# Spreading the S5 Toeplitz tables by SBUF-to-SBUF DMAs from GpSimd instead of one-hot matmuls

## The chip, the cores and the metric

The kernel runs on one core of one Trainium2 chip. The metric is the device time of one execution in microseconds, taken as the median over runs. Beside the timed runs there is one profiled execution, and all rows below come from it.

## What is computed

The reference is a two-layer decoder trunk on 256 positions of width 2048. Layer 0 is an S5 state-space mixer, layer 1 a sparse-attention mixer; both sit between RMS norms with modulation by a vector c. Only the S5 mixer matters here:

```python
u, z = jnp.split(h @ w_in, 2, axis=-1)
ug = u.reshape(B_, L, SSM_GROUPS, SSM_GROUP)        # 128 groups of 16 channels
bu = einsum('blgc,gnc->blgn', ug, bb)               # complex, 64 states per group
x  = scan over l of  x_l = a * x_{l-1} + bu_l       # complex, diagonal
y  = Re(einsum('blgn,gcn->blgc', x, c)) + d_skip * ug
y  = gelu(y); y = y * sigmoid(y @ w_glu + b_glu)
out = (y * silu(z)) @ w_out
```

The scan is cut into blocks of four positions. What the positions of one block do to each other is a small lower-triangular Toeplitz matrix per group (4 by 4 blocks of 16 by 16 numbers). Its first block row, 16 by 64 numbers per group, is the table this case is about.

## The kernel before

Weights stream from DRAM in 512 KB pieces into a ring of eight slots (`raw`, loads issued from SyncE's queue). `split_w` (lines 194 to 206) makes of each half piece a rounded part `hi` on ScalarE (line 203) and a remainder `lo` on VectorE (line 204), and `project_half` (lines 222 to 230) runs three matmuls of 128x256 per weight tile on them, at lines 228, 229 and 230, into the tile `acc`. All large projections go this way.

The S5 mixer interleaves its own work with such projections. `PLAN` is a list of strings, one for each call of `fill()`: "u" is half a projection of u (24 matmuls), "z" half of one of z, "m" a modulation column pair on TensorE and "d" one on VectorE (line 145, two instructions of 128x1024 each on `raw`). The order in the program is `u_turn(0)`, `scan_in(0)`, `scan_run(0)`, `scan_local(0)`, the rest of the u halves, `u_turn(1)`, `scan_in(1)`, `scan_out(0)`, `scan_run(1)`, `scan_local(1)`, `y_turn(0)`, `scan_out(1)`, `y_turn(1)`; the index is the half f of the groups. The framework then lays the instructions of each engine out by when their operands become ready in its model, not strictly in program order; each engine runs its own list in order.

Before them, in a loop over `s` in the order 2, 3, 0, 1, the tables are made: matmuls at line 482 into `kp`, then `kdt[s // 2]` is put together at lines 486, 487 and 491. `kdt[0]` lies in `ey[:, 2048:2560]`, `kdt[1]` in `stab[:, 0:512]`; each holds eight column groups m of 64 numbers. `scan_local(f)` (lines 658 to 679) has for each `g2` two steps. First the table is spread over partitions: for each `hl`, four one-hot matmuls (line 668, lhsT a window of `sel`, 32 rows deep, 128x512 at the widest) write `tzp` in PSUM, and ScalarE copies it (line 670) into `tz`, which lies in `scr` and has one buffer of 128 x 2 x 8 x 64 numbers. Then 32 small matmuls per `hl` (line 676, `tp`) apply `tz` to `U`, and ScalarE writes the result back into `U` (line 678). A `fill()` follows. `sel` is built on GpSimd at lines 433 and 435.

Around it: `scan_run(f)` (lines 627 to 656) is a chain of VectorE operations at lines 634 to 637 and 655 to 656. `cact`, which line 145 reads, is loaded by GpSimd's queue (line 534) and passed through Silu on ScalarE (line 535). `pick` (lines 537 and 538) and `turn` (line 542) are one-hot tables that GpSimd builds; `u_turn` (line 556) needs `pick`. `load_ct(1)` (line 624) loads 2 MB through GpSimd's queue for `scan_out(1)`.

Of the kernel before, what the change touches and what calls it, by code (L numbers as in the profile page):

```python
# [11 lines left out]
AF = mybir.ActivationFunctionType  # L12
# [60 lines left out]
def trunk_kernel(ctx, tc, xT, crow, ccol, vec, m0n, mn, mt, w_ur, w_in, w_glu, w_out, w_kv, w_qr, w_q, w_g,  # L73
                 w_z, w_o, cw1, cw2, b2row, lam, lstep, bmat, cmat, dvec, outT):
    nc = tc.nc
# [13 lines left out]
    def psb(shape, name):  # L89
        return ps2.tile(shape, F32, tag="sm", name=name)  # L90
# [35 lines left out]
    stab = pool.tile([128, 2112], F32, tag="stab", name="stab")  # L126
# [297 lines left out]
    id32 = stab[:, 1920:1952]  # L424
# [3 lines left out]
    V.tensor_reduce(par, id32.rearrange("p (e c) -> p e c", e=2), axis=AX.X, op=OP.add)  # L428
    id16 = stab[:, 1856:1872]
    V.tensor_add(id16, id32[:, 0:16], id32[:, 16:32])  # L430

    sel = stab[:, 640:816]
    nc.gpsimd.memset(sel, 0.0)
    for e in range(2):
        nc.gpsimd.tensor_copy(sel[:, 48 + 64 * e:64 + 64 * e], id32[:, 16 * e:16 * e + 16])
    kdt = [ey[:, 2048:2560], stab[:, 0:512]]
    kdt = [t.rearrange("p (m n) -> p m n", m=8) for t in kdt]

# [16 lines left out]
    for s in (2, 3, 0, 1):  # L455
# [19 lines left out]
        for x in range(4):  # L475
            for g2 in range(2):
                pr = slice(64 * g2, 64 * g2 + 64)
                for ql in range(2):
                    h = 2 * x + ql
                    o = 64 * g2 + 32 * ql  # L480
                    for r in range(2):
                        nc.tensor.matmul(kp[o:o + 32, x].rearrange("p b m -> p (b m)"),
                                         bb[r][pr, 32 * h:32 * h + 32], kc_[pr, 2 * h:2 * h + 2, r, :],
                                         start=(x == 0 and r == 0), stop=True, skip_group_check=True)
# [8 lines left out]
        for q in range(4):  # L493
            p = psb([128, 2, 2, 128], "btp")
# [17 lines left out]
    tz = scr[:, 2944:3968].rearrange("p (l m n) -> p l m n", l=2, m=8)  # L512

    def powers():
        for t, a in zip(QW, (PR, PI)):
            V.tensor_copy(t[:, 0, :], a[:, :, 3])
        for n in (1, 2, 4):
            d = [[t[:, n + x, :] for t in QW] for x in range(n)]
            for x in range(0, n):
                ar, ai = [t[:, x, :] for t in QW]  # L520
                br, bi = [t[:, n - 1, :] for t in QW]
                u1, u2 = w1[:, 0:64], w2_[:, 0:64]
                V.tensor_mul(u1, ar, br)
                V.tensor_mul(u2, ai, bi)
                V.tensor_sub(d[x][0], u1, u2)
                V.tensor_mul(u1, ar, bi)
                V.tensor_mul(u2, ai, br)
                V.tensor_add(d[x][1], u1, u2)
        for t, i in zip(SG, (0, 7)):
            V.tensor_scalar(t[:, 0, :], QW[1][:, i, :], -1.0, None, op0=OP.mult)  # L530
            V.tensor_copy(t[:, 1, :], QW[1][:, i, :])

    powers()
    nc.gpsimd.dma_start(cact, crow.to_broadcast((128, D)))
    nc.scalar.activation(cact, cact, AF.Silu)
# [57 lines left out]
    def fill():  # L593
        for c in PLAN[slot[0]]:
            {"u": u_half, "z": z_half, "m": pe_mod, "d": dve_mod, "c": lambda: cmp_next(), "q": lambda: q_rows()}[c]()
        slot[0] += 1
# [61 lines left out]
    def scan_local(f):  # L658

        bs = slice(8 * f, 8 * f + 8)  # L660
        kt = kdt[f].rearrange("p m (d c) -> p m d c", d=4)
        for g2 in range(2):
            for hl in range(2):

                pr = slice(64 * g2 + 32 * hl, 64 * g2 + 32 * hl + 32)
                p = psb([128, 8, 4, 16], "tzp")
                for j in range(4):
                    nc.tensor.matmul(p[:, :, j:4, :], sel[pr, 48 - 16 * j:176 - 16 * j], kt[pr, :, 0:4 - j, :],
                                     start=(j == 0), stop=(j == 3), skip_group_check=True)
                nc.scalar.activation(tz[:, hl], p.rearrange("p m j c -> p m (j c)"), AF.Copy)  # L670
            for hl in range(2):
                p = psb([128, 8, 64], "tp")
                for m in range(8):
                    for e in range(2):
                        pr = slice(64 * e, 64 * e + 64)
                        nc.tensor.matmul(p[pr, m, :], tz[pr, hl, m, :], U[pr, 8 * f + m, 2 * g2 + hl, :],
                                         start=(m == 0), stop=True, skip_group_check=True)
                nc.scalar.activation(U[:, bs, 2 * g2 + hl, :], p, AF.Copy)
            fill()

    def scan_out(f, cts):
# [35 lines left out]
    scan_in(0)  # L717
    scan_run(0)
    scan_local(0)
    fill()  # L720
    fill()
# [4 lines left out]
    scan_out(0, load_ct(0))  # L726
    scan_run(1)
    scan_local(1)
    y_turn(0)
    yhl = Act(["va", "vb"], "yhl")  # L730
# [147 lines left out]
    def cmp_next():  # L878
        e, i = divmod(ncmp[0], 4)
        if e < 2 and nblk[0] >= 4 * e + 4:  # L880
            cmp_piece(e, i)
            ncmp[0] += 1
# [5 lines left out]
    def q_rows():  # L888
        k = nrow[0]
        if k == KT or ncmp[0] < 8:  # L890
            return
        nrow[0] += 1
        if k == 0:
            hq[0] = Act(["ha"], "hq")
            qacc.extend([psb([128, 2, L], "qacc%d" % i) for i in range((QN + 1) // 2)])
        while npe[0] < NA + min(NB, 2 * k + 2):
            pe_mod()
        if 2 * k >= NB:
            while ndve[0] < 48 - NA + 2 * k + 2 - NB:
                dve_mod()  # L900
            c = modv[:, 48 + k:65 + k:16]
            V.tensor_add(c, c, modw[:, 16 + k:33 + k:16])
            V.tensor_add(c, c, vecs[:, VOFF["mb"][0] + 48 + k:VOFF["mb"][0] + 65 + k:16])
        V.scalar_tensor_tensor(scol1[:, k:k + 1], in0=modv[:, 64 + k:65 + k], scalar=1.0, in1=vv_("g1", k, k + 1),
                               op0=OP.add, op1=OP.mult)
        norm_mod(x, rstd1, scol1, modv[:, 48:64], hq[0], (k,))
        r = raw_tile("qraw")
        nc.sync.dma_start(r[:, 0:QN, :], w_qr[k].rearrange("p (a b) -> p a b", b=128))
        w = split_w(r, QN)
        for i in range(QN):  # L910
            hi, lo = w[i // 4]
            acc = qacc[i // 2][:, i % 2, :]
            nc.tensor.matmul(acc, hi[:, i % 4, :], hq[0](0, k), start=(k == 0 and i % 2 == 0), stop=False,
                             skip_group_check=True)
            nc.tensor.matmul(acc, hi[:, i % 4, :], hq[0](1, k), start=False, stop=False, skip_group_check=True)  # L915
            nc.tensor.matmul(acc, lo[:, i % 4, :], hq[0](0, k), start=False, stop=(k == KT - 1),
                             skip_group_check=True)
# [38 lines left out]
    for h in range(4):  # L956
# [8 lines left out]
        for k in range(4):  # L965
            kt = 4 * h + k
# [5 lines left out]
    p = psb([128, 2, 48], "gp")  # L972
# [15 lines left out]
    for h in range(16):  # L988
        kv = h // 4
        pn = []  # L990
        for qh in range(2):
# [17 lines left out]
            for br in range(2):  # L1009
                o = 16 + n * br  # L1010
# [64 lines left out]
    for m in range(0, 16, 2):  # L1075
        e = nc.gpsimd if m in (6, 12) else V
# [91 lines left out]
```

## Time and profile before

| what | value |
|---|---|
| median of 3 runs | 1360.05 us (1359.97 to 1362.2) |
| profiled execution, its own time | 1356.18 us |
| its span (first to last instruction) | 1354.5 us |
| busy: TensorE matmul, VectorE, ScalarE, GpSimd | 1267.1, 1056.9, 688.1, 21.7 us |
| `scan_local(0)` and `scan_local(1)` begin | 189.7 and 284.8 us |

PE is TensorE's matmul row, PEld its weight loads, DVE VectorE, ACT ScalarE, POOL GpSimd, SP SyncE. Times in rows are microseconds from the span's start unless marked ns. "L668" is line 668 of the kernel. A releaser behind an arrow is what ended an idle time. PEclk is the clock that was granted to TensorE as a share of 2.4 GHz; 0.5 is 1.2 GHz. Successive matmuls overlap, so the distance from one group's start to the next group's start says more than a duration.

### The profile page before, as it was taken

How to read it: one execution, taken by the hardware profiler on the slowest of the kernel's cores; microseconds unless marked ns; L12 is line 12 of the kernel's file. 1: busy time of each engine (PE TensorE's matmuls, PEld its weight loads, DVE VectorE, ACT ScalarE, POOL GpSimd, SP SyncE). 2: the span in 40 equal slices, each digit the busy share in tenths (PEclk: the TensorE clock that was granted, in tenths of full speed). 3: DMA queues.
4: the chain of work that ended last, by engine and by line, in shares of the span. 5: the costliest groups of instructions: out<-in, count | busy, mean ns of one | idle time of the engine just before them, and what ended most of it. 6: DMA issues, size and time to landing. Idle time of an engine off the chain costs nothing.

```text
span 1354.5 us, 31620 instructions
## 1 busy us (share of the span) xinstructions
PE 1267.1 (94%) x12526; PEld 1203.9 (89%) x12526; DVE 1056.9 (78%) x2291; ACT 688.1 (51%) x1463; POOL 21.7 (2%) x47
## 2 busy tenths in 40 slices
PE   2799999999889999998999899999999999999995
PEld 1678888888789999997999899999999999999995
DVE  5999769799768787659997878777888777776665
ACT  3345543437435555445455445555555565555653
POOL 2000000000100000000000000000000000000001
PEclk9899998999899999997999999999999999999998
DMA  9799954545879899869998789876555444444541
GB/s 342 259 384 316 350 194 147 212 138 197 295 280 362 299 344 327 309 232 385 322 352 272 241 278 326 273 253 216 175 199 192 149 154 145 154 143 154 187 157 62
DMA packets 93253, 331.05 MB, mean 244 GB/s; under 512 B 12512, under 2 KB 12672, under 8 KB 92080
## 3 DMA queue, kind: packets, MB, share of 16 engines
q1 hardware_dynamic: 91792, 321.45, 67.8%
q0 software_dynamic: 1312, 7.58, 1.5%
q8 instruction: 98, 1.61, 0.5%
q14 instruction: 51, 0.42, 0.1%
HBM read 324.79 MB, written 4.19 MB: 243 GB/s over the span
## 4 chain that ended last, share of the span: by engine, by line
PE 62%; DMA 4%; DVE 3%; issue 1%; ACT 1%; DVEq 0%; ACTq 0%
PE acc L230 18%; PE acc L229 18%; PE acc L228 18%; DMA raw<-in_mt_dram 3%; PE s L1002 1%; DVE lo L204 1%; PE op L1053 1%; PE macc L158 1%; PE op L1050 1%; DMA raw<-in_w_kv_dram 1%; DVE raw L145 1%; PE op L1054 1%; PE cp L838 0%; PE qacc L915 0%; PE cp L839 0%
## 5 line engine op out<-in xcount | busy, mean ns | idle before, releaser
L203 ACT ACTIVATE hi<-raw 128x512 fp32r<-128x512 f32 x640 | 400.0, 630 | 450.7 <-PE acc L229 388.6
L204 DVE TENSOR_TENSOR lo<-raw,hi 128x512 fp32r<-128x512 f32 x640 | 433.2, 688 | 154.5 <-ACT hi L203 148.2
L229 PE MATMUL acc<-hq,hi 128*128 128x256 f32 x960 | 274.6, 286 | 0.0
L228 PE MATMUL acc<-hq,hi 128*128 128x256 f32 x960 | 273.1, 285 | 0.4 <-ACT hi L203 0.4
L230 PE MATMUL acc<-hq,lo 128*128 128x256 f32 x960 | 271.0, 284 | 1.5 <-DVE lo L204 1.3
L145 DVE SCALAR_TENSOR_TENSOR raw<-raw,ey 128x1024 f32<-128x1024 f32 x156 | 189.9, 1220 | 63.0 <-DMA raw<-in_mt_dram 57.3
L229 PEld LDWEIGHTS acc<-hq,hi 128*128 128x128 f32 x960 | 181.0, 189 | 3.7 <-issue 3.3
L230 PEld LDWEIGHTS acc<-hq,lo 128*128 128x128 f32 x960 | 180.4, 189 | 3.5 <-DVE lo L204 2.1
L228 PEld LDWEIGHTS acc<-hq,hi 128*128 128x128 f32 x960 | 181.0, 189 | 1.2 <-issue 0.7
L230 PE MATMUL acc<-h,lo 128*128 128x256 f32 x384 | 112.3, 294 | 9.4 <-DVE lo L204 9.3
L230 PE MATMUL acc<-hkv,lo 128*128 128x256 f32 x384 | 112.3, 293 | 4.5 <-DVE lo L204 4.3
L228 PE MATMUL acc<-hkv,hi 128*128 128x256 f32 x384 | 112.0, 292 | 0.9 <-ACT hi L203 0.9
L228 PE MATMUL acc<-h,hi 128*128 128x256 f32 x384 | 112.8, 294 | 0.0
L229 PE MATMUL acc<-hkv,hi 128*128 128x256 f32 x384 | 111.0, 289 | 0.0
L229 PE MATMUL acc<-h,hi 128*128 128x256 f32 x384 | 110.2, 287 | 0.0
L230 PEld LDWEIGHTS acc<-h,lo 128*128 128x128 f32 x384 | 74.5, 195 | 12.4 <-DVE lo L204 11.4
L230 PEld LDWEIGHTS acc<-hkv,lo 128*128 128x128 f32 x384 | 76.1, 198 | 6.1 <-DVE lo L204 5.8
L158 PE MATMUL macc<-mraw,cz 128*32 128x128 f32 x1600 | 56.5, 292 | 24.4 <-DMA mraw<-in_m0n_dram 19.8
L228 PEld LDWEIGHTS acc<-hkv,hi 128*128 128x128 f32 x384 | 76.4, 199 | 1.5 <-ACT hi L203 1.5
L228 PEld LDWEIGHTS acc<-h,hi 128*128 128x128 f32 x384 | 74.6, 194 | 2.9 <-issue 0.8
L229 PEld LDWEIGHTS acc<-hkv,hi 128*128 128x128 f32 x384 | 76.4, 199 | 0.0
L229 PEld LDWEIGHTS acc<-h,hi 128*128 128x128 f32 x384 | 74.7, 195 | 0.0
(339 smaller groups left out, 2808.3 us busy)
## 6 DMA issues: line engine op xcount, KB each, us to landing
raw<-in_mt_dram SPq DMA_DIRECT2D x156, 512.0 KB, 5.8
raw<-in_w_z_dram SPq DMA_DIRECT2D x96, 512.0 KB, 3.8
mraw<-in_m0n_dram SPq DMA_DIRECT2D x64, 512.0 KB, 8.0
raw<-in_w_in_dram SPq DMA_DIRECT2D x48, 512.0 KB, 5.3
raw<-in_w_kv_dram SPq DMA_DIRECT2D x48, 512.0 KB, 6.2
mraw<-in_mn_dram SPq DMA_DIRECT2D x36, 512.0 KB, 6.1
raw<-in_w_glu_dram SPq DMA_DIRECT2D x32, 512.0 KB, 6.6
raw<-in_w_out_dram SPq DMA_DIRECT2D x32, 512.0 KB, 5.9
```

Of the source, the lines that this page charges most:

```text
L145: nc.vector.scalar_tensor_tensor(out=rf, in0=rf, scalar=1.0, in1=cact[:, 1024 * e:1024 * e + 1024], op0=OP.mult, op1=OP.mult, accum_out=mo ...
L158: nc.tensor.matmul(acc[32 * j:32 * j + 32, 128 * e:128 * e + 128], cz[:, q, :], r[:, q % 8, :], start=(e == 0 and q < 4), stop=(q >= 12), ...
L203: nc.scalar.activation(hi[:, 0:c, :], rr, AF.Copy)
L204: nc.vector.tensor_sub(lo[:, 0:c, :], rr, hi[:, 0:c, :].bitcast(F32))
L228: nc.tensor.matmul(acc, hi[:, kk, :], act(0, k), start=(k == 0), stop=False)
L229: nc.tensor.matmul(acc, hi[:, kk, :], act(1, k), start=False, stop=False)
L230: nc.tensor.matmul(acc, lo[:, kk, :], act(0, k), start=False, stop=(k == KT - 1))
L1002: nc.tensor.matmul(sp, qo(a, h)[:, qs], kk[:, kv, b, o:o + w], start=(i == 0), stop=(i == 2))
L1050: nc.tensor.matmul(op_, vc[0:15, kv, :], tcm[0:15, :], start=True, stop=True)
L1053: nc.tensor.matmul(op_, vt[:, kv, br - 1, 0, :], t[:, 0:256], start=True, stop=False)
L1054: nc.tensor.matmul(op_[:, 128:256], vt[:, kv, br - 1, 1, :], t[:, 256:384], start=False, stop=True)
```

## The change

The one-hot matmuls, their PSUM tile and its copy on ScalarE go, and with them `sel`. In their place `load_tz(f, g2)` issues 16 DMAs from GpSimd's queue (two `hl`, two `e`, four `j`); each copies 16 partitions of the table to 16 partitions of `tz`, shifted right by 16 j columns. `tz` is cleared once. The runs are 256, 192, 128 and 64 bytes long for j = 0 to 3, eight of them per partition (for j = 0 they lie one behind the other on both sides). The first load is issued before `powers()`, each later one after the `tp` matmuls that read the tables before it, into the same buffer. `u_turn` stays as it is.

```diff
-    sel = stab[:, 640:816]
-    nc.gpsimd.memset(sel, 0.0)
-    for e in range(2):
-        nc.gpsimd.tensor_copy(sel[:, 48 + 64 * e:64 + 64 * e], id32[:, 16 * e:16 * e + 16])
...
+    nc.gpsimd.memset(tz, 0.0)
+
+    def load_tz(f, g2):
+
+        for hl in range(2):
+            for e in range(2):
+                i = 64 * g2 + 32 * hl + 16 * e
+                for j in range(4):
+                    o = 64 * e + 16 * j
+                    nc.gpsimd.dma_start(tz[o:o + 16, hl, :, 16 * j:64], kdt[f][i:i + 16, :, 0:64 - 16 * j])
+
+    load_tz(0, 0)
     powers()
     nc.gpsimd.dma_start(cact, crow.to_broadcast((128, D)))
...
-        kt = kdt[f].rearrange("p m (d c) -> p m d c", d=4)
         for g2 in range(2):
-            for hl in range(2):
-
-                pr = slice(64 * g2 + 32 * hl, 64 * g2 + 32 * hl + 32)
-                p = psb([128, 8, 4, 16], "tzp")
-                for j in range(4):
-                    nc.tensor.matmul(p[:, :, j:4, :], sel[pr, 48 - 16 * j:176 - 16 * j], kt[pr, :, 0:4 - j, :],
-                                     start=(j == 0), stop=(j == 3), skip_group_check=True)
-                nc.scalar.activation(tz[:, hl], p.rearrange("p m j c -> p m (j c)"), AF.Copy)
             for hl in range(2):
...
                 nc.scalar.activation(U[:, bs, 2 * g2 + hl, :], p, AF.Copy)
+            if 2 * f + g2 < 3:
+                load_tz(f + g2, 1 - g2)
             fill()
```

## Rows read from the trace of the kernel before

**Rows 1.** The page's head: span, and busy time of each engine.
```profile
span 1354.5 us, 31620 instructions
PE 1267.1 (94%) x12526; PEld 1203.9 (89%) x12526; DVE 1056.9 (78%) x2291; ACT 688.1 (51%) x1463; POOL 21.7 (2%) x47
```
**Rows 2.** Busy time by stretch: us, busy (instructions) of each engine, clock, DMA share, GB/s.
```profile
189.72:246.23 56.51, 53.71 (x463) 49.37 (x462) 55.66 (x102) 23.03 (x42) 0.00 (x0) 0.91 0.52 174
284.75:340.93 56.18, 55.45 (x580) 48.88 (x579) 52.69 (x99) 35.92 (x59) 0.00 (x0) 0.97 0.53 192
```
**Rows 3.** Who waited for whom, 160 to 341 us: total, times, longest.
```profile
PE acc L230 <- DVE lo L204: 3.5, 4, 2.4
```
**Rows 4.** Busy time by stretch, columns as in Rows 2: a group of `scan_in`, then around the spreads.
```profile
179.95:181.79 1.84, 1.84 (x66) 1.77 (x65) 0.92 (x2) 0.89 (x2) 0.00 (x0) 1.00 0.50 191
...
189.72:193.68 3.96, 3.96 (x17) 2.47 (x16) 3.92 (x7) 1.49 (x3) 0.00 (x0) 1.00 0.43 141
193.68:196.47 2.79, 2.79 (x13) 2.56 (x12) 2.75 (x6) 0.70 (x2) 0.00 (x0) 0.52 0.50 176
...
198.80:203.26 4.46, 4.46 (x40) 4.32 (x37) 4.36 (x8) 1.87 (x4) 0.00 (x0) 1.00 0.01 3
...
189.72:198.80 9.08, 9.08 (x93) 7.29 (x93) 8.98 (x16) 3.32 (x6) 0.00 (x0) 0.81 0.53 174
203.26:212.34 9.08, 9.08 (x94) 7.29 (x93) 8.98 (x16) 3.32 (x6) 0.00 (x0) 0.81 0.35 113
284.75:293.83 9.08, 9.08 (x93) 7.29 (x93) 8.87 (x18) 3.32 (x6) 0.00 (x0) 0.81 0.68 262
298.30:305.88 7.58, 7.58 (x93) 5.89 (x92) 7.42 (x14) 3.74 (x7) 0.00 (x0) 1.00 0.43 141
```
**Rows 5.** Line 670 on ScalarE, its instructions and durations (ns min/median/max).
```profile
L670 ACT ACTIVATE scr<-tzp x8: 590/598/605, 192.2 to 302.4; 128x512 f32<-128x512 f32 x8
```
**Rows 6.** Line 145 alone in the first stretch of Rows 2: us, DVE busy (instructions).
```profile
189.72:246.23 56.51, 12.05 (x20) 0.91 0.52 174
```
**Rows 7.** GpSimd in order of time: start, us, line, operation [idle before <-releaser].
```profile
2.11 1.06 POOL L130 DMA_DIRECT2D stab<-in_lstep_dram  x2
...
53.83 2.05 POOL L435 COPY stab<-stab 128x16 f32<-128x16 f32 x2
72.47 0.58 POOL L466 DMA_DIRECT2D ctd<-ctA  x1 [16.60 <-DVE ctA L453]
...
143.86 0.35 POOL L537 MEMSET stab<- 128x272 f32 x1
...
282.32 1.06 POOL L624 DMA_DIRECT2D ct<-ctd  x2 [137.66 <-issue]
```
**Rows 8.** DMA issues on GpSimd's queue: count, KB each, median us from issue to landing.
```profile
ct<-ctd POOLq DMA_DIRECT2D x2, 1024.0 KB, 8.7
...
l<-in_cw_dram POOLq DMA_DIRECT2D x1, 128.0 KB, 2.4
...
stab<-in_lstep_dram POOLq DMA_DIRECT2D x2, 16.0 KB, 5.9
```
**Rows 9.** VectorE in order of time, where `kdt[0]` is finished.
```profile
142.81 0.22 DVE L516 COPY scr<-stab 128x64 f32<-128x64 f32 x1 [1.38 <-PE kp L482]
...
161.89 1.22 DVE L145 SCALAR_TENSOR_TENSOR raw<-raw,ey 128x1024 f32<-128x1024 f32 x1 [1.43 <-ACT ey L535]
...
163.04 0.22 DVE L491 TENSOR_TENSOR ey<-ey,dg 128x64 f32<-128x64 f32 x1
```
**Rows 10.** TensorE in order of time: `scan_out(0)` and `scan_out(1)` begin.
```profile
271.25 1.97 PE L692 MATMUL yp<-Vva,ctA 64*64 64x64 f32 x62
...
340.93 0.91 PE L692 MATMUL yp<-Vvb,ct 64*64 64x64 f32 x22
```
**Rows 11.** Busy time by stretch: VectorE around GpSimd's issue at 72.47; TensorE after an idle time.
```profile
60.00:92.00 32.00, 28.56 (x460) 24.60 (x450) 31.96 (x45) 14.02 (x33) 1.10 (x2) 1.00 0.98 371
...
159.37:162.94 3.57, 3.57 (x17) 3.57 (x18) 2.14 (x6) 3.56 (x7) 0.00 (x0) 0.54 0.90 343
```
**Rows 12.** The one copy on VectorE in `scan_run(0)`.
```profile
212.17 0.23 DVE L643 COPY scr<-Vva 128x64 f32<-128x64 f32 x1
```

## The prediction

> **What bounds the kernel now.** I read the page's head first: TensorE is busy 94% of the span, VectorE 78%, GpSimd 2% [rows 1]. That is an average, so next came the two stretches that hold the spreads [rows 2]. From 189.72 to 246.23 TensorE is busy 53.7 of 56.5 us and VectorE 55.7 of 56.5; from 284.75 to 340.93 it is 55.5 and 52.7 of 56.2. Both are nearly full; which one ends waits last is in the list of waits: between 160 and 341 us TensorE stood for VectorE's `lo` only 3.5 us in 4 waits [rows 3], and no wait of TensorE there is on a DMA. So TensorE sets the pace here, with VectorE close behind, and in the first stretch 12.1 us of VectorE's time is line 145 [rows 6], modulation work that is put where there is room.
>
> **What goes from TensorE.** A spread (one `g2`, both `hl`) takes 3.96 us from its start to the start of the next group; there are four: 15.8 us. The stretches behind them show more [rows 4]. While the first spread runs, the granted clock reads 1.00; in the 2.79 us behind it, with 12 projection matmuls, it reads 0.52, the 1.2 GHz level. Twelve such matmuls need 1.49 us at full clock (36 of them took 4.46), and 64 records of the shape of `tp` (`scan_in`'s, 64x64) took 1.84 [rows 4]. So of the 9.08 us from the first spread's start to the end of its `tp` group only 1.49 + 1.84 = 3.33 are needed without the spread, and 5.75 go. The second and third spread have the same 9.08 us; the fourth, whose clock stays at 1.00, has 7.58 [rows 4] and gives 4.25. Sum: 3 x 5.75 + 4.25 = 21.5 us off TensorE's list, 11.5 for f = 0 and 10.0 for f = 1.
>
> ScalarE loses eight copies of 0.60 us [rows 5]; it is 51% busy [rows 1] and I count nothing. GpSimd loses `sel` (2.05 us for two copies [rows 7]), which nobody waits for at that time.
>
> **What is added.** 64 DMAs on GpSimd's queue. An issue takes 0.53 us (two `lstep` loads in 1.06, 64 runs of 256 bytes each) to 0.58 us (`ctd` store) [rows 7]. I take 0.56, so one `load_tz` needs 16 x 0.56 = 9.0 us of GpSimd, 36 us in all, on an engine that stood 137.7 us before 282.32 [rows 7]. From the last issue to landing: 2.4 us (`cw`, 128 KB) to 5.9 (`lstep`, the one with runs of 256 bytes, but issued at the start beside other loads) [rows 8]. I take 2.4, as DMA shares of 0.52 and 0.53 [rows 2] leave room; 5.9 stays as the upper end. A load is then 11.4 us (upper 14.9). The bytes (0.33 MB a load) are less than one of the 512 KB weight pieces, so I count nothing for bandwidth.
>
> Where does this lie? *First load.* `kdt[0]` is finished at 163.3 us [rows 9], so `tz` is there at 174.7 (upper 178.2), 11 us or more before 189.7. In the program it stands ahead of the `cact` load, `pick` and `turn` on GpSimd. Were it ahead of them in the queue too, these would wait from 143.9 [rows 7] to 172 us. But the trace's order goes by readiness: line 516, written after line 491, runs at 142.81, and line 491 at 163.04, after the first line 145, which already needs `cact` [rows 9]. I therefore leave `cact` ahead. The clearing of `tz` can precede it: a 272-column memset took 0.35 us [rows 7], so 1024 columns some 1.3 us (estimate). Behind it waits the first line 145, which waits for `cact` anyway (1.43 us [rows 9]); its cover is the projection work that TensorE has by then. Nothing counted.
>
> *Third load* (f = 1, g2 = 0): issued when the last `tp` of f = 0 has read `tz`, before 212, and read by the `tp` that now comes after 284.75 [rows 4]. Even 20 us earlier that leaves 50. Hidden.
>
> *Second and fourth load.* These wait until `tp` of the same f has read `tz`, and the next `tp` group waits for them. In the order of before there are 48 projection matmuls between the two `tp` groups, 48 x 0.124 = 6.0 us. If the order stays, TensorE stands 11.4 - 6.0 = 5.4 us, and after an idle time the clock is at the lower level: 17 matmuls took 3.57 us at 0.54 [rows 11] where 17 x 0.124 = 2.1 are needed, so 1.5 us more. That makes 6.9 us for a load, 13.8 for both; with the upper landing 10.4 and 20.8. If the order moves, other projection halves fill the time, and it is 0: behind the first `tp` group of f = 0 there are still twelve u halves (`PLAN` from its fifth entry) of 24 x 0.124 = 3.0 us, none of which needs `tz`, and the result is not read before `scan_out(0)` at 271 [rows 10]. The trace speaks for that: 12 projection matmuls lie between each spread and its `tp`, covering the copy into `tz` [rows 4]. A misjudged landing would leave a rest, so I take 3.5 us, half of one wait. The 2 MB of `load_ct(1)` go through the same queue just before the fourth load [rows 7], and land 8.7 us later (median) [rows 8], by 293; the last issue of the fourth load would be near 296, so they don't delay it.
>
> *GpSimd beside a busy VectorE.* The `ctd` issue took 0.58 us while VectorE was busy 31.96 of 32 us [rows 7, 11]; the two `sel` copies, tiny ones, took 2.05 [rows 7]. The issue is the nearer row. The Trainium skill (SBUF — State Buffer, SBUF: two separate sides) warns that GpSimd cannot write its DMA descriptors while VectorE runs an operation in a two-port mode, such as an fp32 copy in SBUF. By that rule a single operation in `scan_run(0)` would block, a copy of 0.23 us [rows 12], and the sum would not move; read as a rule about any busy VectorE, it gives the second rival below.
>
> *VectorE.* In the first stretch it needs 55.7 us; less line 145 it is 43.6, and 56.5 - 11.5 = 45.0 us remain. If line 145 stays there, f = 0 gains only 0.9 us; if it moves, all 11.5. As it is filler, I take near the second, less 2.8 us, which is what TensorE idles in this stretch now (56.5 - 53.7 [rows 2]).
>
> **The sum.** -21.5 + 2.8 + 3.5 = -15.2 us. The profiled execution took 1356.18 us (1354.5 of span [rows 1] and 1.7 around it), 3.9 below the median of 1360.05; its counterpart would be 1341.0, the median 1360.05 - 15.2 = 1344.9, say 1345.
>
> **The rivals.** *The order stays, and TensorE waits twice for `tz`.* For it: each engine runs a fixed list, and a modelled landing can be too early. -21.5 + 2.8 + 13.8 = -4.9 us, 1355; with the upper landing +2.1, 1362. *GpSimd's issues are stretched by VectorE, and the kernel is slower.* Place: second and fourth load. Price: at 1.03 us per issue, the `sel` copies' pace [rows 7], a load takes 16.4 + 2.4 = 18.8 us, a wait is 12.9 and 1.5 for the clock, both 28.7: -21.5 + 2.8 + 28.7 = +10, 1370. It decides against the change once both waits pass 18.7 us, which is an issue of 0.71 us. Against it: the `ctd` row. *VectorE sets the pace of f = 0.* Line 145 does not move, and the 11.5 shrink to 0.9: -10.9 + 3.5 = -7.4, 1353. That the spread would still be done on TensorE is excluded by the diff.
>
> **Chances.** The forecast 0.62; the order stays 0.16, half of it at the lower wait; stretched issues 0.15; VectorE 0.07. About 0.2% (2.7 us) is what a measurement can tell from no change. Faster by more: 0.62 + 0.08 + 0.07, less a little for forecasts that come out short = 0.74. Within: 0.10. Slower: 0.16. The forecast's own range is 1337 (all 21.5 and a little of the present 2.8 us of waits) to 1352. For 8 in 10 I go down to 1336 and up to 1361, short of the stretched issues and of the longest waits.
>
> **What would show it.** Right: no `tzp` rows; granted clock 1.00 through `scan_local`; `scan_out(1)` starts some 15 us before 341 [rows 10]; more projection matmuls than 48 between the `tp` groups; 64 issues of 0.5 to 0.6 us on GpSimd. Wrong: TensorE idle before `tp` on a DMA into `tz`; issues near 1 us; VectorE still full to 246 with line 145 inside and TensorE waiting for `lo`; `cact` or `pick` late at 160 to 175 us.

## The result, and the profile after

The changed kernel takes 1342.7 us (median; 1339.97 to 1347.5) beside 1360.53 us of the kernel before: a ratio of 0.9882, 95% interval 0.9859 to 0.9905. Timed a second time it gave 1342.15 us beside 1356.81, ratio 0.9881 (0.9846 to 0.9916). By the ratio that is 16 us less, where 15 had been forecast; the medians alone differ by 17.8 and 14.7 us. The profiled execution took 1339.97 us, 1338.2 of it span. Its page's head, beside [rows 1]:

```profile
span 1338.2 us, 31587 instructions
...
PE 1254.2 (94%) x12462; PEld 1193.8 (89%) x12462; DVE 1053.9 (79%) x2291; ACT 686.0 (51%) x1457; POOL 54.5 (4%) x109
```

TensorE is busy 12.9 us less and has 64 matmuls less; GpSimd is busy 33 us more. The line numbers have moved: `u_turn` is line 563, the load 537, the `tp` matmuls 674, `scan_run` 641 to 644 and 662 to 663, `scan_out` 692.

Busy time by stretch in the kernel after (columns as in [rows 2]): the stretch from the first `tp` group to `u_turn(1)`, which answers to the first of [rows 2]; then `u_turn(1)` to `scan_out(0)` in two parts; the wait in `scan_out(0)` and what follows it; and from the first `tp` of f = 1 on.

```profile
189.38:234.88 45.50, 43.10 (x431) 40.89 (x430) 40.54 (x68) 20.34 (x37) 16.61 (x32) 1.00 0.76 247
234.88:245.40 10.52, 10.52 (x147) 5.27 (x148) 10.01 (x32) 3.90 (x7) 0.00 (x0) 1.00 0.42 150
245.40:268.54 23.14, 21.58 (x424) 20.61 (x417) 22.93 (x29) 10.47 (x27) 0.00 (x0) 1.00 0.28 93
...
268.54:278.22 9.68, 9.68 (x149) 9.43 (x149) 9.61 (x17) 0.64 (x2) 1.12 (x2) 0.65 0.31 81
...
278.22:333.70 55.48, 53.38 (x684) 49.02 (x684) 55.07 (x110) 35.99 (x58) 8.30 (x16) 1.00 0.69 230
```

Two things stand here. The first stretch shrank from 56.51 to 45.50 us, and the clock in it is 1.00 where it was 0.91: that is the gain. But from 245.40 on VectorE is busy 22.93 of 23.14 us, and in the 9.68 us behind it the granted clock is 0.65: that is a loss the kernel before does not have. Who waited, 160 to 345 us (beside [rows 3]):

```profile
PE acc L230 <- DVE lo L204: 3.0, 5, 1.4
PE yp L692 <- DVE Vva L663: 1.6, 1, 1.6
PE acc L228 <- ACT hi L203: 1.4, 1, 1.4
```

No wait of TensorE is on a DMA into `tz`. The wait at L692 is new. VectorE waits too. Its waits in the first stretch, first in the kernel before (189.72 to 246.23), then in the kernel after (189.38 to 234.88):

```profile
DVE raw L145 <- DMA raw<-in_mt_dram: 0.3, 1, 0.3
```

```profile
DVE raw L145 <- DMA raw<-in_mt_dram: 5.2, 5, 2.3
```

These are weight pieces that line 145 reads and that had not landed. GpSimd in order of time, beside [rows 7] (the loads are `scr<-ey` for f = 0, `scr<-stab` for f = 1):

```profile
143.19 1.00 POOL L528 MEMSET scr<- 128x1024 f32 x1 [51.35 <-PE kp L477]
144.15 0.53 POOL L541 DMA_DIRECT2D ey<-in_crow_dram  x1
...
163.93 4.73 POOL L537 DMA_DIRECT2D scr<-ey  x9 [18.30 <-DVE ey L486]
168.91 0.54 POOL L537 DMA_DIRECT2D scr<-ey  x1 [0.25 <-DMA scr<-ey]
170.45 2.60 POOL L537 DMA_DIRECT2D scr<-ey  x5 [1.00 <-DMA scr<-ey]
174.06 0.53 POOL L537 DMA_DIRECT2D scr<-ey  x1 [1.01 <-DMA scr<-ey]
...
190.82 4.15 POOL L537 DMA_DIRECT2D scr<-ey  x8 [16.23 <-PE tp L674]
...
196.93 3.65 POOL L537 DMA_DIRECT2D scr<-ey  x7 [0.35 <-issue]
203.85 4.15 POOL L537 DMA_DIRECT2D scr<-stab  x8 [3.28 <-PE tp L674]
215.94 4.15 POOL L537 DMA_DIRECT2D scr<-stab  x8 [7.94 <-PE tp L674]
274.05 1.12 POOL L631 DMA_DIRECT2D ct<-ctd  x2 [53.96 <-PE yp L692]
279.65 3.67 POOL L537 DMA_DIRECT2D scr<-stab  x7 [4.48 <-PE tp L674]
285.36 4.67 POOL L537 DMA_DIRECT2D scr<-stab  x9 [2.03 <-DMA scr<-stab]
```

Eight issues take 4.15 us, 0.52 us each, and `cact` (L541) stayed ahead of the first load. Within a load GpSimd stands now and then until one of its own DMAs has landed. These are waits of the program: in the trace each issue waits on one of eight semaphores in turn, the one that the DMA eight places before it reports to. The tenth issue starts at 168.91, behind the landing of the second at 168.63, and the sixteenth at 174.06, behind that of the eighth at 173.78. The landings, beside [rows 8] (count, KB each, median us), and from issue to landing over all 64:

```profile
scr<-ey POOLq DMA_DIRECT2D x8, 32.0 KB, 4.7
...
scr<-stab POOLq DMA_DIRECT2D x8, 8.0 KB, 3.6
```

```profile
DMA to landing us min/median/max: 1.7/4.2/8.0
```

From its first issue to its last landing the first load takes 16.9 us (163.93 to 180.81), the second 12.7 (190.82 to 203.50) and the fourth 13.2 (279.65 to 292.82); the third waits in its middle for `tp`.

The `tp` groups on TensorE in order of time, between and behind which projection matmuls run; the last three rows are `scan_out(0)`, beside [rows 10]:

```profile
189.38 2.09 PE L674 MATMUL tp<-U,scr 64*64 64x64 f32 x64
...
197.53 0.33 PE L674 MATMUL tp<-U,scr 64*64 64x64 f32 x2
...
202.52 1.14 PE L674 MATMUL tp<-U,scr 64*64 64x64 f32 x30
...
214.60 0.56 PE L674 MATMUL tp<-U,scr 64*64 64x64 f32 x12
...
259.90 3.77 PE L692 MATMUL yp<-Vva,ctA 64*64 64x64 f32 x128
...
266.64 0.33 PE L692 MATMUL yp<-Vva,ctA 64*64 64x64 f32 x4
...
268.54 5.21 PE L692 MATMUL yp<-Vva,ctA 64*64 64x64 f32 x124 [1.57 <-DVE Vva L663]
```

The second `tp` group no longer follows as a block: it is spread from 197.5 on, with projection work between, and no wait for `tz` shows in it.

To see where the span went, it is cut at instructions that every kernel has: the first `ut`, the start of the local part of f = 1 (its first `tzp`, or its first `tp` where there is none; 278.22 in the kernel after), the first `acc<-yhl` (start of w_glu), the first `acc<-hkv` (start of the K/V stage) and the last `acc<-hkv`. In the kernel after the other rows are:

```profile
L563 PE MATMUL ut<-x,stab x128: 592/592/617, 165.9 to 241.4; 128*32 128x512 f32 x128
...
L228 PE MATMUL acc<-yhl,hi x256: 280/283/387, 389.2 to 485.3; 128*128 128x256 f32 x128
...
L228 PE MATMUL acc<-hkv,hi x384: 277/283/580, 601.4 to 811.6; 128*128 128x256 f32 x192
...
L230 PE MATMUL acc<-hkv,lo x384: 278/283/561, 603.0 to 811.8; 128*128 128x256 f32 x192
```

The table has the same for each kernel that was run. "S5" is from the first `ut` to the first `acc<-hkv`; "to f = 1" and "to w_glu" are its first two parts, and what is left of it is w_glu and w_out. "K/V" is from the first `acc<-hkv` to the start of the last. The last column is VectorE's wait at line 145 for weight pieces (`raw`) in K/V. Ratios are to the kernel before, timed beside it.

| kernel | ratio (95% interval) | to f = 1 | to w_glu | S5 us | K/V us | line 145 waits |
|---|---|---|---|---|---|---|
| before | 1 | 118.4 | 127.6 | 457.7 | 205.4 | 17.3 |
| after | 0.9882 (0.9859 to 0.9905) | 112.3 | 111.0 | 435.5 | 210.4 | 20.7 |
| after_again | 0.9881 (0.9846 to 0.9916) | 113.3 | 112.2 | 437.8 | 212.4 | 21.0 |
| both | 1.0014 (0.9991 to 1.0036) | 120.9 | 130.9 | 462.0 | 202.3 | 14.0 |
| dma_f0 | 0.9899 (0.9876 to 0.9921) | 110.5 | 123.4 | 442.6 | 206.7 | 20.3 |
| dma_f1 | 0.9903 (0.9887 to 0.9919) | 118.7 | 116.4 | 444.7 | 211.4 | 20.2 |
| deep | 0.9955 (0.9937 to 0.9972) | 112.3 | 127.5 | 452.6 | 208.7 | 19.2 |
| noload | 0.9808 (0.9773 to 0.9843) | 105.4 | 120.6 | 437.0 | 200.2 | 12.2 |
| noload_again | 0.9782 (0.9755 to 0.9808) | 104.9 | 119.2 | 438.0 | 201.1 | 13.3 |
| twice | 0.9951 (0.9925 to 0.9977) | 110.1 | 114.2 | 447.2 | 212.3 | 23.8 |
| fewer_d | 0.9741 (0.9715 to 0.9768) | 103.5 | 112.6 | 427.7 | 203.1 | 16.5 |
| before_fewer_d | 1.0046 (1.0028 to 1.0064) | 120.0 | 133.9 | 465.3 | 207.2 | 17.9 |
| kvorder | 0.9855 (0.9840 to 0.9870) | 110.4 | 115.1 | 437.3 | 208.6 | 17.4 |
| kvorder_again | 0.9821 (0.9794 to 0.9848) | 110.7 | 115.2 | 438.6 | 203.8 | 14.5 |

Two executions of one program differ by 1.0 to 2.3 us in S5 and by up to 4.8 in K/V (kvorder), which bounds what a single row can tell. From the last `acc<-hkv` to the last `acc<-hq`, the projections behind K/V, it is 416 to 419 us in all of them. What lies ahead of the first `ut` takes 164.5 to 170.7 us, in the two executions of the kernel after 165.9 and 170.7, so times within S5 are compared from its start.

So S5 gained 22.2 us (19.9 in the second execution), and the K/V stage, which the change does not touch, gave 5.0 (7.0) of that back. Of the 22.2 (19.9), 6.1 (5.1) lie ahead of f = 1 and 16.6 (15.4) between there and w_glu.

### The profile page after: what moved, and what is told of

It reads as the page before. It is cut to its first block, busy times and chain, and to the rows that moved or that the text cites. A ratio compares the mean times of both kernels' runs of the same rounds, so it can differ in the third digit from the quotient of the medians.

```text
span 1338.2 us, 31587 instructions
## 1 busy us (share of the span) xinstructions
PE 1254.2 (94%) x12462; PEld 1193.8 (89%) x12462; DVE 1053.9 (79%) x2291; ACT 686.0 (51%) x1457; POOL 54.5 (4%) x109
## 4 chain that ended last, share of the span: by engine, by line
PE 72%; DVE 13%; DMA 10%; issue 3%; ACT 1%; SPq 0%; DVEq 0%; ACTq 0%
PE acc L230 19%; PE acc L228 19%; PE acc L229 19%; DMA raw<-in_mt_dram 7%; DVE lo L204 3%; DVE raw L145 2%; PE macc L158 1%; PE s L1002 1%; DMA mraw<-in_m0n_dram 1%; PE ut L563 1%; PE op L1053 1%; DMA uraw<-in_w_ur_dram 1%; PE op L1050 1%; PE vp L616 1%; PE kp L477 1%
## 5 line engine op out<-in xcount | busy, mean ns | idle before, releaser
L228 PE MATMUL acc<-h,hi 128*128 128x256 f32 x384 | 110.7, 289 | 1.9 <-ACT hi L203 1.4
L229 PE MATMUL acc<-h,hi 128*128 128x256 f32 x384 | 108.5, 283 | 0.0
L158 PE MATMUL macc<-mraw,cz 128*32 128x128 f32 x1600 | 59.2, 296 | 24.6 <-DMA mraw<-in_m0n_dram 19.6
L228 PEld LDWEIGHTS acc<-h,hi 128*128 128x128 f32 x384 | 73.1, 190 | 4.0 <-ACT hi L203 1.8
L158 PEld LDWEIGHTS macc<-mraw,cz 128*32 128x32 f32 x1600 | 45.6, 118 | 33.0 <-issue 19.2
```

Source lines behind the costliest of these rows:

```text
L158: nc.tensor.matmul(acc[32 * j:32 * j + 32, 128 * e:128 * e + 128], cz[:, q, :], r[:, q % 8, :], start=(e == 0 and q < 4), stop=(q >= 12), ...
L228: nc.tensor.matmul(acc, hi[:, kk, :], act(0, k), start=(k == 0), stop=False)
L229: nc.tensor.matmul(acc, hi[:, kk, :], act(1, k), start=False, stop=False)
```

## The experiments

**The second execution.** The changed kernel once more.

> The changed kernel once more, beside the other three. Both theories: near 1343 us against 1360.5 before.

0.9881 and 435.5 against 437.8 us: the result holds.

**The matmuls back beside the loads.** The loads stay, and the one-hot matmuls run as well, their result unread.

```diff
+            for hl in range(2):
...
+                p = psb([128, 8, 4, 16], "tzp")
+                for j in range(4):
+                    nc.tensor.matmul(p[:, :, j:4, :], sel[pr, 48 - 16 * j:176 - 16 * j], kt[pr, :, 0:4 - j, :],
+                                     start=(j == 0), stop=(j == 3), skip_group_check=True)
```

> The changed kernel with the one-hot matmuls put back on TensorE as well; they write PSUM and nobody reads it, tz still comes by DMA, and ScalarE's copies stay out. Theory (TensorE's 15.8 us in the spreads plus 5.7 at the lower clock are the gain): all of it comes back, 1358 to 1364. Rival (the gain is a better order of the work, or the copies on ScalarE and the wait for them): stays near the changed kernel, 1343 to 1348.

1.0014, S5 462.0 us: the whole gain is gone, and 4.3 us more than in the kernel before. What the change earns, it earns by those matmuls' absence; the loads themselves bring nothing, and neither does the absence of ScalarE's copies, which stay out here.

**One half each.** `dma_f0` loads only f = 0 by DMA and keeps the one-hot matmuls for f = 1; `dma_f1` the reverse.

```diff
+            for hl in range(2 if f == 1 else 0):
+                p = psb([128, 8, 4, 16], "tzp")
...
-            if 2 * f + g2 < 3:
+            if f == 0 and g2 == 0:
```

> Loads by DMA for f = 0 only, one-hot matmuls for f = 1. The stretch from the first u_turn matmul to the first hkv projection was 457.7 us before and 435.5 after. Theory (the time saved on TensorE counts where it is saved): 11 us shorter than before, about 446; if the late end of scan_run(0) takes its 4.8 us, about 451. Rival (the gain comes from the tail of S5 alone): 456 or more.

> Loads by DMA for f = 1 only, one-hot matmuls for f = 0. Theory (the time saved on TensorE counts where it is saved): the stretch from the first u_turn matmul to the first hkv projection is 10 us shorter than the 457.7 before, about 448. Rival (the f = 1 part is covered by the chain through scan_run(1)): 455 or more.

S5 fell by 15.1 and 13.0 us, both more than the 11 and 10 that stood against them, and their sum is 28, where the whole change gives 20 to 22. Up to w_glu the halves do add up: there they give 12.1 and 10.9, together 23.0, and the whole change 22.7 and 20.5. The other 3.0 and 2.1 us lie in w_glu and w_out, behind all spreads and loads, where the kernel after has nothing of the kind (212.2 us, 211.7 before); two executions of one program differ there by up to 2.9 (`noload`), and the cause is not shown. The trace of `dma_f0` has the wait of `scan_out(0)`, that of `dma_f1` does not. Who waited, 160 to 345 us, in `dma_f0`:

```profile
PE yp L706 <- DVE Vva L668: 1.5, 1, 1.5
```

That wait therefore comes with the spreads of f = 0 leaving TensorE. It does not show as a loss in the sum: `dma_f0` is 7.9 us shorter up to f = 1, and 4.2 us shorter from there to w_glu, although the spreads of f = 1 are still in that part.

**The clock alone.** In the kernel before, the one-hot matmuls read 128 rows instead of 32.

```diff
-                    nc.tensor.matmul(p[:, :, j:4, :], sel[pr, 48 - 16 * j:176 - 16 * j], kt[pr, :, 0:4 - j, :],
+                    nc.tensor.matmul(p[:, :, j:4, :], sel[:, 48 - 16 * j:176 - 16 * j], kt[:, :, 0:4 - j, :],
```

> The kernel before with its one-hot matmuls 128 rows deep instead of 32 (same columns, same count); each table is then the sum of four, so the local part of the S5 scan is not the reference's. Theory (of the gain 5.7 us is the clock that falls behind the shallow matmuls): the granted clock stays at 1.00 behind the spreads, and from a spread's start to the end of its tp group it takes 7.3 us instead of 9.1; the stretch from the first u_turn matmul to the first hkv projection is 5 to 6 us shorter than the 457.7 before. Rival (the clock falls there for another reason, such as the wait for the copy into tz): 9.1 us and 457.7 as before.

Busy time around the first spread (192.1 to 196.2) and behind it, columns as in [rows 4]:

```profile
192.10:196.20 4.10, 4.10 (x16) 2.51 (x16) 4.07 (x8) 1.50 (x3) 0.00 (x0) 1.00 0.46 140
196.20:199.00 2.80, 2.80 (x53) 2.66 (x53) 2.80 (x6) 1.23 (x2) 0.00 (x0) 1.00 0.58 181
```

The spread costs about the same time (4.10 us, 3.96 before), but in the 2.80 us behind it the granted clock is 1.00, and the 12 projection matmuls are followed by some 40 of `tp`; in the kernel before the 12 alone took 2.79 at 0.52 [rows 4]. TensorE in order of time, around the first spread of `deep`:

```profile
192.05 4.48 PE L668 MATMUL tzp<-ey,stab 128*128 128x512 f32 x16
...
197.89 2.08 PE L676 MATMUL tp<-U,scr 64*64 64x64 f32 x64
199.90 0.39 PE L228 MATMUL acc<-h,hi 128*128 128x256 f32 x1
```

From the spread's start to the end of its `tp` group that is 7.85 us (7.3 expected), and the same at the other three, where it was 9.08 three times and 7.58 [rows 4]: together 3.4 us. S5 is 5.1 us shorter, for the 5.7 of the prediction (21.5 less the 15.8 of the spreads), all of it ahead of f = 1; there a wait of 2.44 us for `lo` at 218.5 us in the kernel before is gone as well. So 3.4 to 5.1 of the 21.5 us were the clock behind the shallow matmuls. A kernel with deep matmuls and the right table was not run.

**What the loads cost.** `noload` issues none (`tz` stays cleared); `twice` issues each of them two times.

```diff
-    load_tz(0, 0)
...
-            if 2 * f + g2 < 3:
-                load_tz(f + g2, 1 - g2)
```

```diff
-                    nc.gpsimd.dma_start(tz[o:o + 16, hl, :, 16 * j:64], kdt[f][i:i + 16, :, 0:64 - 16 * j])
+                    for _ in range(2):
+                        nc.gpsimd.dma_start(tz[o:o + 16, hl, :, 16 * j:64], kdt[f][i:i + 16, :, 0:64 - 16 * j])
```

> The changed kernel with all 64 loads of tz left out; tz stays zero, so the local part of the S5 scan is missing from the output. Theory (the gain is TensorE's time for the spreads, and the loads are hidden behind projections): within 3 us of the changed kernel, 1340 to 1346. Rival (the second and fourth load hold TensorE or GpSimd's issues slow VectorE down): 7 us or more faster than the changed kernel, about 1335.

> Every load of tz is issued twice, 32 issues per load instead of 16, some 17 us of GpSimd for a load. Theory (hidden, there are over 30 us of other projection work behind each tp group): at most 3 us more than the changed kernel, 1343 to 1346. Rival (the issues are on the path of the second and fourth load): 8.3 us more for each, about 1359.

> The kernel without the loads of tz (tz stays zero, so the Toeplitz products of S5 are left out in value) once more, for the K/V stage: from the first to the last acc<-hkv it took 200.2 us, where the changed kernel took 210.4 and 212.4. If that is the kernel's own (its order of work there), it comes to 199 to 202 again, and the time to 1330 to 1335. If it differs from execution to execution of one program, it comes to 205 or more, with a time of 1337 or more.

In total `noload` is 10 to 12 us faster than the changed kernel, which is the figure of the rival. The cause that the rival names does not show: no wait of TensorE is on `tz`, and an operation of line 145 takes 1.22 us with the loads and without. Cut by stage, the loads are not cleared either. S5 takes 437.0 and 438.0 us without any load, 435.5 and 437.8 with them. That equality is made of two differences: without loads S5 is 7 to 8 us shorter up to f = 1 (105.4 and 104.9 against 112.3 and 113.3) and 7 to 10 us longer from there to w_glu (120.6 and 119.2 against 111.0 and 112.2). The order of TensorE's work differs as well: in `noload` the second `tp` group is one block again, and in the first stretch line 145 waits 1.4 us for its pieces instead of 5.2. So the loads cost S5 nothing in sum, and no wait names them; what they cost by way of the order is not separated. The difference in the total lies in K/V (200.2 and 201.1 against 210.4 and 212.4), some 300 us behind the last load. It belongs to the program: both kernels were timed twice, and the medians are 1332.34 and 1330.02 against 1342.7 and 1342.15.

`twice` missed too: S5 is 9.4 to 11.7 us longer, where nearly nothing had been expected. The issues of one load then take 20 to 25 us, the last of all starts at 301.6 where it was at 289.5, and nearly the whole loss lies behind the first `acc<-yhl` (222.9 us from there to K/V, 212.2 in the kernel after). Here too the order changed: 22 projection matmuls that the kernel after has ahead of that point lie behind it (2.7 us at 0.124 each), and TensorE waits 6.5 us for `lo` there instead of 2.2. The other 3.7 us were not traced, nor whether late tables or the new order cause it.

**VectorE's order ahead of `scan_out(0)`.** Three "d" (six operations of line 145, each of which leaves two records) are taken out of the two steps behind `scan_local(0)`, ahead of `scan_out(0)`, and put into empty steps of the w_glu loop; in the changed kernel, and, as a control, in the kernel before.

```diff
-    "ud", "ud", "ud", "ud", "uu", "uu", "uuuud", "uuuudd", "zd", "z", "zd", "z", "z", "z", "zz", "zz",
+    "ud", "ud", "ud", "ud", "uu", "uu", "uuuu", "uuuu", "zd", "z", "zd", "z", "z", "z", "zz", "zz",
...
-    "d", "", "d", "d", "", "d", "d", "", "d", "d", "m", "d", "d", "", "d", "d",
+    "d", "d", "d", "d", "d", "d", "d", "d", "d", "d", "m", "d", "d", "", "d", "d",
```

> The changed kernel with three of the VectorE pieces of other weights (letter d of PLAN) taken out of the two steps ahead of scan_out(0) and put into empty steps of the w_glu loop. In the trace of the changed kernel TensorE waited 1.57 us at 268.54 for scan_run(0)'s last step on VectorE (Vva, L663) and ran at a granted clock of 0.63 to 0.66 until 278.22. Theory: the order of VectorE there was the loss, so the wait and the low clock shrink or vanish, the stretch from u_turn(0)'s first matmul to the first acc<-hkv falls from 435.5 (437.8 in the second execution) to 431 to 434, and the time comes to 1336 to 1340. Rival: the pieces are late where they now stand (w_glu and w_out wait for them), the stretch stays at 435 to 438 and the time at 1341 to 1344.

> The kernel before (one-hot matmuls, no loads) with the edit of PLAN that took the changed kernel from 435.5 to 427.7 us in the stretch from u_turn(0)'s first matmul to the first acc<-hkv and from 0.988 to 0.974 of the time. In the kernel before TensorE did not wait for scan_run(0)'s last step at scan_out(0). Theory: the edit repairs a wait that the change itself made, so that here the stretch stays within 3 us of 457.7, and the time comes to 0.993 to 1.000 of before, what it gains being in the K/V stage (205.4 us before, 200 to 203 with this order there). Rival: the edit gains the same with or without the change; the stretch falls by 8 or more, to 450 or less, and the time to 0.985 to 0.988.

1325.16 us beside 1359.11 of the kernel before, ratio 0.9741: the gain of 16 us became 34 to 35, the best time of all kernels here. Line 145 alone from 186 to 235 us, first the kernel after, then `fewer_d`:

```profile
186.00:235.00 49.00, 12.29 (x20) 1.00 0.74 241
```

```profile
186.00:235.00 49.00, 4.92 (x8) 1.00 0.66 209
```

And `scan_run`'s last operations on VectorE (ns min/median/max, first and last start), first the kernel after, then `fewer_d`:

```profile
L663 DVE TENSOR_TENSOR Vva<-Vva,scr x8: 1083/1088/1093, 245.4 to 267.4; 128x896 f32<-128x896 f32 x8
```

```profile
L663 DVE TENSOR_TENSOR Vva<-Vva,scr x8: 1085/1092/1093, 241.2 to 258.4; 128x896 f32<-128x896 f32 x8
...
L692 PE MATMUL yp<-Vva,ctA x256: 218/218/267, 260.4 to 270.7; 64*64 64x64 f32 x128
```

With 7.4 us less of line 145 the chain ends at 259.5, 89.1 us behind the first `ut` (170.4), instead of 268.5, 102.6 behind it (165.9). That is ahead of `scan_out(0)` at 260.4, which then runs through in 10.3 us and not 13.5, and from its start to the first `tp` of f = 1 (273.9) it is 13.5 us, as in the kernel before. S5 is 427.7 us, 7.8 to 10.1 less than in the changed kernel and more than the theory asked (431 to 434), all of it ahead of f = 1 (103.5 us for 112.3); the other 7 to 9 us of the gain lie in K/V, where this kernel takes 203.1, for a reason that is not shown. The six pieces also leave the DMA queues in that stretch, where line 145 now waits 2.1 us and not 5.2; VectorE's work and its waits for pieces are not told apart. In the kernel before the same edit makes S5 7.6 us longer and the time 0.5% longer; there the chain ended 13 us ahead of `scan_out(0)`, as its last operations show, with `scan_out(0)` at 271.25 [rows 10]:

```profile
L656 DVE TENSOR_TENSOR Vva<-Vva,scr x8: 1083/1089/1093, 220.8 to 257.1; 128x896 f32<-128x896 f32 x8
```

So the edit does not gain by itself; it repairs what the change had made late. The control missed its theory's numbers (within 3 us, 0.993 to 1.000) on the slow side: TensorE's waits for `lo` from 165 to 345 us are 8.3 us where they were 4.4, and 6.3 of the 7.6 us lie between f = 1 and w_glu (133.9 for 127.6); the rest was not traced.

**The K/V stage.** One "m" (a group of modulation matmuls) moves from a step of w_out to the step behind it, which gives TensorE, from there on, nearly the order that `noload` has.

```diff
-    "d", "m", "d", "", "d", "d", "", "m", "d", "", "d", "", "d", "", "", "",
-    "mmmm",
+    "d", "m", "d", "", "d", "d", "", "", "d", "", "d", "", "d", "", "", "",
+    "mmmmm",
```

> The changed kernel with one modulation pair on TensorE moved from the w_out stage to its end; S5 and w_glu keep the order of the changed kernel, and the K/V stage is laid out for 5042 of its last 5500 TensorE instructions as in the kernel without loads. Theory (the changed kernel gives 5 to 7 us back in the K/V stage by the order of that stage, not by the loads): from first to last hkv projection 200 to 203 us instead of 210 to 212, the whole about 1334. Rival (the K/V stage varies from run to run, or the loads reach into it): 210 us there, 1342.

> The changed kernel with one module matmul group (letter m of PLAN) moved from a step of w_out to the step after its end, once more. Its first profile had 208.6 us from the first to the last acc<-hkv (210.4 and 212.4 in the changed kernel, 200.2 and 202.3 in two kernels with nearly the same order of TensorE there). If the order of TensorE sets that stage, this execution should fall nearer to 202; if the stage differs by what else is under way, it stays at 206 to 212. The time: 1338 to 1342 either way by its first timing.

208.6 and 203.8 us: the first near the rival's 210, the second near the theory's 203, and 5 us apart for one program. The time fell by 0.3% and 0.6% below that of the changed kernel; the second median, 1335.34, is below the 1338 to 1342 expected. What the table does show is that K/V is long where line 145 waits long for weight pieces. Who waited, over K/V, first the kernel after, then `noload`:

```profile
DVE raw L145 <- DMA raw<-in_mt_dram: 20.7, 12, 3.5
```

```profile
DVE raw L145 <- DMA raw<-in_mt_dram: 12.2, 12, 2.9
```

The kernels with TensorE's order of the changed one there (after in both executions, twice, dma_f1) wait 20 to 24 us and take 210 to 212; `noload` (both executions) and `both`, which share another, wait 12 to 14 and take 200 to 202. That the order sets the give-back is not shown: `fewer_d` and `kvorder` have nearly the order of `noload`, and `kvorder` still waited 17.4 us and took 208.6 in one execution, 14.5 and 203.8 in the other. Why the pieces come later in some executions than in others stays open.

## Why the prediction was right, and where it was not

The forecast of 1345 was met (1342.7), and its main term is borne out. That the rest of the sum came to the right number is luck.

*TensorE's 21.5 us.* Right. There are no `tzp` rows, the clock is 1.00 from 189.38 to 234.88, and `both` brings all of it back. `deep` measured the clock's part: 3.4 us at the spreads themselves, 5.1 in S5, for 5.7.

*Issue and landing.* An issue took 0.52 us (0.56 taken), the memset 1.00 (1.3). From issue to landing it was 4.2 us in the median and 1.7 to 8.0 in all, not 2.4: the row of `cw`, one wide load from DRAM, was the wrong neighbour, and the truth lay nearer to the `lstep` row. Not foreseen was that an issue waits for the landing of the DMA eight places before it. So the issues of the first load went from 163.93 to 174.59, 10.7 us, and its last landing came at 180.81, later than the forecast's upper end (178.2), but still 8.6 us ahead of the first `tp`. Two of the other loads took 12.7 and 13.2 us, between the forecast's 11.4 and 14.9.

*Waits for `tz`: 3.5 taken, none measured.* The order moved, as the forecast had it, and far enough. The rival in which it stays would have needed TensorE idle before `tp`; the waits hold no such row.

*GpSimd beside a busy VectorE.* From 279.65 to 290.03 VectorE is busy 10.28 of 10.38 us, and the sixteen issues in it take 8.30, 0.52 each. The rival of stretched issues (1.03) is refuted for this mix of operations. The warning of the Trainium skill (SBUF — State Buffer, SBUF: two separate sides) speaks of operations in a two-port mode, such as an fp32 copy. VectorE's operations in that time are tensor-tensor ones and a single copy of 0.23 us, and no issue of these loads took longer than 0.56 us, so this case hardly tests it.

*VectorE.* Here the step failed. It said that line 145 is filler and moves out of the first stretch, less 2.8 us. It did not move: 20 records and 12.1 us of it lie in that stretch before [rows 6], and the window after has as many:

```profile
189.38:234.88 45.50, 12.09 (x20) 1.00 0.76 247
```

What moved out is the end of the chain of `scan_run(0)`. VectorE's busy time in the stretch fell from 55.66 us [rows 2] to 40.54, and the chain's last operations, which began at 220.8 in the kernel before, begin at 245.4 in the kernel after. VectorE runs its list in order, and on top of line 145's own 12.1 us stand the 5.2 us in which it waited for pieces.

The rival "VectorE sets the pace of f = 0" had the premise that line 145 stays, with a price of 10.6 us in that stretch. The stretch shrank by 11.0 us in spite of it, and the chain was late at the far end instead. From the start of `scan_out(0)` to the first `tp` of f = 1 the kernel after needs 278.22 - 259.90 = 18.3 us, before it was 284.75 - 271.25 = 13.5: 4.8 us, of which 1.57 is the wait and the rest mostly the clock of 0.65 behind it. `fewer_d`, with 13.5 there, shows that this was what VectorE had ahead of it. Where the lateness falls is not fixed: both executions of `kvorder`, whose TensorE and VectorE have the same order in S5 as the kernel after, need 14.4 and 14.0 us there and lose time earlier. Over all four, S5 up to f = 1 is 5.1 to 8.0 us shorter than before, where TensorE's term for f = 0 was 11.5.

*What the sum did not have.* Between f = 1 and w_glu the kernel after is 16.6 us shorter (15.4 in the second execution), where the spreads of f = 1 stood for 10.0. In that part TensorE stood 10.7 us in the kernel before, at a mean clock of 0.96, and 3.6 us in the kernel after, at 1.00; first the window of before, then that of after:

```profile
284.75:412.30 127.55, 116.85 (x1433) 106.56 (x1433) 100.92 (x195) 65.23 (x114) 3.58 (x13) 0.96 0.69 249
```

```profile
278.22:389.20 110.98, 107.38 (x1402) 99.26 (x1402) 103.16 (x200) 65.28 (x112) 12.89 (x29) 1.00 0.83 300
```

So what was short of 11.5 ahead of f = 1 (5.4 and 6.4 us) is about what this part gave beyond 10.0 (6.6 and 5.4), and S5 as a whole gave 22.2 and 19.9 us, about TensorE's full 21.5. The 6.3 us that the forecast took off that (2.8 and 3.5) were not paid in S5. What brought the total down to 16 was the K/V stage, which gave back 5.0 to 7.0 us in a part of the kernel that the prediction never looked at, for a reason that is still open.

## What to carry to other kernels

When work is taken off the engine that sets the pace, follow the chain of the next busy engine to where its result is read, not only to the end of the stretch: here VectorE's filler stayed, the chain behind it was late some 80 us further on, and moving six operations took another 8 to 10 us off S5 (and as much off K/V, unexplained). Price such a move again after the change; the same edit cost half a per cent before it. A total alone misleads, and so does one stage: without the loads the total was 10 us shorter and S5 no shorter, but S5's two parts differed by 7 us and more in opposite directions, and the order of the work had changed along with the loads. A kernel with a part left out is a clean comparison only where the order of the rest is the same.

## What the hardware showed that was not expected

- Behind three of the four spreads with matmuls 32 rows deep the granted clock fell, behind the first to 0.52 over 2.79 us, although TensorE had been busy throughout [rows 4]. With the same ones 128 rows deep (`deep`) it stayed at 1.00 behind all four, in nearly the same time for a spread (4.24 us, 3.96 before).
- GpSimd issued a DMA in 0.50 to 0.56 us, 0.52 each beside a VectorE that was busy 10.28 of 10.38 us.
- DMAs of 8 to 32 KB from SBUF to SBUF landed 1.7 to 8.0 us after their issue, 4.2 in the median. In this program each issue waits for the landing of the one eight places before it, so a long series goes slower than its issues: the 32 of the first load in `twice` took 24.8 us, 163.82 to 188.64, where 32 times 0.52 is 16.6.
